# Batched matmul: x of two batches per transfer, the first x as one transfer, transposes of a pair in one block

## The chip, the cores and the metric

One Trainium2 chip, one core. The metric is the device time of one execution in microseconds (us). Most executions of a kernel agree within 0.3%. With one core there is no second die to compare, so slow runs would show only as runs over 1.5% above the fastest.

## The reference

```python
def setup_inputs():
    batch, m, k, n = 32, 512, 1024, 768
    return {"x": randn(batch, m, k).astype(float32), "weight": randn(batch, k, n).astype(float32)}

def reference(x, weight):
    return np.matmul(x, weight).astype(np.float32)
```

Per batch the kernel must read 2.10 MB of x and 3.15 MB of weights and write 1.57 MB of output: 218 MB in 32 batches.

## The kernel before

x and weights are loaded by transfers that cast float32 to bf16 on the way (issued by the GpSimd queue); the first x alone comes as float32, by the SyncE queue. A row group of x is 4 rows of one partition, 16 KB in memory; of the weights 8 rows, 24 KB. The TensorE transposes x in pairs of bf16 values taken as float32 words, the VectorE copies the result from PSUM to SBUF, and the matmuls follow. The parts that the change touches:

```python
x_pool  = ctx.enter_context(tc.tile_pool(name="x", bufs=5))
xT_pool = ctx.enter_context(tc.tile_pool(name="xT", bufs=8))
# ...
def load_x(b):
    xs[b] = x_pool.tile([P, MT, K], BF16, name="x_sb")
    nc.gpsimd.dma_start(out=xs[b], in_=x_view[b])

def transpose(b, mt):
    pt = tpsum.tile([P, JT, P], F32, name="pt")
    pairs = xs[b].bitcast(F32)
    for j in range(JT):
        nc.tensor.transpose(pt[:, j, :], pairs[:, mt, j::JT], ident)
    xT = xT_pool.tile([P, JT, P, 2], BF16, name="xT")
    nc.vector.tensor_copy(...)                     # contiguous
    return xT
# ...  the first x: three of four rows of each partition, then 18 small transfers
x_first = first_pool.tile([P, MT, K], F32)
nc.sync.dma_start(x_first[:, :MT - 1], x_view[0, :, :MT - 1])
at = 0
for few, times in ((4, 2), (5, 1), (6, 1)):
    for _ in range(times):
        for first in range(at, at + 4):
            rows = slice(first, at + 4 * few, 4)
            nc.sync.dma_start(x_first[rows, MT - 1], x_view[0, rows, MT - 1])
        at += 4 * few
for rows in (slice(at, 80), slice(80, P)):
    nc.sync.dma_start(x_first[rows, MT - 1], x_view[0, rows, MT - 1])
# ...  in the loop over batches: transposes stand between the matmul groups
xT = {mt: turn(b, mt) for mt in (0, 1)}
for pair in range(2):
    pm = banks()
    for half in range(2):
        if pair == 0:
            matmuls(pm, half, xT[half], b, range(KT), False)
            xT[2 + half] = turn(b, 2 + half)
        else:
            matmuls(pm, half, xT[2 + half], b, range(KT), False)
    evacuate(b, pair, pm)
```

The last outputs are held back and stored at the end, so that the DMA engines have work while the last batches are computed.

## Time and profile before

| | before |
|---|---|
| time, median (range) of the first 6 runs | 516.93 us (516.89 to 516.97) |
| profiled span | 515.2 us |
| TensorE busy | 81% |
| bytes moved at the memory | 218.1 MB, 423 GB/s over the span |
| first transpose | 33.6 us |
| last TensorE work ends | about 501.2 us |

Lines of the page of the kernel before. The three rows are the span in 40 slices, a digit being the busy share in tenths (PEclk: the granted TensorE clock); the last line sums the memory traffic.

```profile
PE   0039999999999988798978879977898978989980
PEclk9999999999999989799988997998997989999995
DMA  8999999999999999999999999999999999999996
HBM read 167.77 MB, written 50.33 MB: 423 GB/s over the span
```

The DMA row has no gap between the first and the last slice, while the TensorE, idle in the first two slices, is less than 90% busy in most slices from the fifteenth (180 us) on. The windows view of the kernel before says the same more finely. After the stretch and its length come the busy times of the engines, then the granted clock, the share of the DMA engines and GB/s.

```profile
100.00:200.00 100.00, 93.19 (x589) 61.67 (x588) 29.66 (x45) 16.98 (x29) 11.14 (x21) 0.98 1.02 270
200.00:300.00 100.00, 85.88 (x516) 55.69 (x515) 24.83 (x38) 15.22 (x26) 10.07 (x19) 0.93 1.02 263
300.00:400.00 100.00, 83.65 (x494) 53.73 (x493) 24.61 (x38) 14.05 (x24) 10.09 (x19) 0.91 1.02 263
505.00:514.00 9.00, 0.00 (x0) 0.00 (x0) 0.00 (x0) 0.00 (x0) 0.00 (x0) 0.50 0.64 267
```

The DMA share is 1.02: packets follow one another without a gap and overlap a little. Only the last stretch falls off, because the 16 engines do not end together.

What the TensorE waited for in the kernel before (us in total, times, longest us):

```profile
PE pm L101 <- DMA w_sb<-in_weight_dram: 44.0, 18, 4.0
PE pt L83 <- DMA x_first<-in_x_dram: 33.6, 1, 33.6
```

It starts late, at 33.6 us: the 18 small transfers of the first x are issued one after another until 25.0 us (the SyncE queue waited ten times, 12.5 us in all, for an earlier one to land), their packets of 172 ns come between weight packets of 926 ns, and the last one lands at 33.6 us. It then still waits 44 us for weights.

### The profile page before, as it was taken

Reading aid. Unit: us, or ns where it says so; the run is one execution under the profiler, and the core shown is the slowest. Engines: PE = TensorE matmul, PEld = TensorE weight load, DVE = VectorE, ACT = ScalarE, POOL = GpSimd, SP = SyncE. Lnnn points to the kernel's source line nnn. Section 1 sums busy time; section 2 is a strip of 40 time slices with the busy share of each in tenths; the row PEclk is TensorE's granted clock in tenths of the full one; section 3 lists DMA queues with packets and bytes.
Section 4 is the critical chain, followed back from the end, with each engine's and each line's share of the span. In section 5 each row is a group of like instructions: output and inputs, shape, how many; then the busy total and the mean of one; then the engine's idle time right before and its main releaser. Section 6 shows DMA issues by size and latency. Waiting matters only on the chain.

```text
span 515.2 us, 6001 instructions
## 1 busy us (share of the span) xinstructions
PE 419.6 (81%) x2576; PEld 275.7 (54%) x2576; DVE 129.8 (25%) x196; ACT 76.2 (15%) x129; POOL 51.7 (10%) x102
## 2 busy tenths in 40 slices
PE   0039999999999988798978879977898978989980
PEld 0026666666666655465645545654564645656650
DVE  0023333333333313133122231322331313332320
ACT  0001111111111101011111111110110111111110
POOL 3000111111000110100101001100111010111000
PEclk9999999999999989799988997998997989999995
DMA  8999999999999999999999999999999999999996
GB/s 233 223 225 220 209 278 277 260 238 276 274 276 267 237 269 276 275 272 245 254 276 275 276 254 243 273 278 275 266 239 265 276 276 274 240 253 213 291 430 272
DMA packets 15081, 135.64 MB, mean 263 GB/s; under 512 B 1744, under 2 KB 1744, under 8 KB 3536
## 3 DMA queue, kind: packets, MB, share of 16 engines
q0 software_dynamic: 13824, 126.88, 96.7%
q1 hardware_dynamic: 1232, 8.39, 4.1%
q8 instruction: 20, 0.33, 0.2%
q14 instruction: 5, 0.04, 0.0%
HBM read 167.77 MB, written 50.33 MB: 423 GB/s over the span
## 4 chain that ended last, share of the span: by engine, by line
DMA 69%; PE 25%; DVE 2%; issue 1%; ACT 0%; POOLq 0%
DMA w_sb<-in_weight_dram 31%; PE pm L101 22%; DMA out_dram<-out_sb 16%; DMA x_sb<-in_x_dram 15%; DMA x_first<-in_x_dram 6%; PE pt L70 2%; PE pt L83 1%; DVE out_sb L113 1%; DVE xT L72 1%; ACT out_sb L112 0%; ACT out_sb L114 0%; POOLq L62 0%; POOLq L148 0%; POOLq L56 0%
## 5 line engine op out<-in xcount | busy, mean ns | idle before, releaser
L101 PE MATMUL pm<-w_sb,xT 128*128 128x256 bf16 (+1 forms) x2048 | 364.7, 336 | 47.9 <-DMA w_sb<-in_weight_dram 44.0
L101 PEld LDWEIGHTS <-xT 128*128 128x128 bf16 x2048 | 203.3, 100 | 184.6 <-issue 50.5
L72 DVE COPY xT<-pt 128x1024 bf16<-128x1024 bf16 x124 | 82.8, 689 | 203.0 <-PE pt L70 203.0
L112 ACT COPY out_sb<-pm 128x512 f32<-128x512 f32 x64 | 37.5, 585 | 286.7 <-PE pm L101 286.7
L70 PEld LDWEIGHTS pt<-ident,x_sb 128*128 128x128 f32 x496 | 72.9, 206 | 6.3 <-issue 1.3
L113 DVE COPY out_sb<-pm 128x512 f32<-128x512 f32 x64 | 44.0, 687 | 128.1 <-PE pm L101 128.1
L70 PE MATMUL pt<-ident,x_sb 128*128 128x128 f32 x496 | 75.4, 286 | 0.0
L114 ACT COPY out_sb<-pm 128x512 f32<-128x512 f32 x64 | 37.5, 586 | 138.2 <-PE pm L101 138.0
L62 POOL DMA_DIRECT2D w_sb<-in_weight_dram x37 | 19.8, 534 | 154.9 <-PE pm L101 74.6
L56 POOL DMA_DIRECT2D x_sb<-in_x_dram x31 | 16.5, 532 | 173.4 <-DMA w_sb<-in_weight_dram 129.4
L83 PE MATMUL pt<-ident,x_first 128*128 128x128 f32 x32 | 6.0, 350 | 33.6 <-DMA x_first<-in_x_dram 33.6
L148 POOL DMA_DIRECT2D out_dram<-out_sb x28 | 15.0, 536 | 93.2 <-DMA x_sb<-in_x_dram 55.9
L83 PEld LDWEIGHTS pt<-ident,x_first 128*128 128x128 f32 x32 | 5.0, 204 | 34.3 <-issue 33.6
L84 DVE CAST xT<-pt 128x512 bf16<-128x512 f32 x8 | 5.6, 726 | 40.7 <-PE pt L83 40.5
L112 ACT ACT_TABLE_LOAD x1 | 1.3, 1283 | 0.7 <-PEq L199 0.7
masks.py:199 POOL TENSOR_SCALAR_AFFINE_SELECT ident<-ident 128x128 f32<-128x128 f32 x1 | 0.3, 287 | 0.1
masks.py:197 POOL MEMSET ident<- 128x128 f32 x1 | 0.2, 223 | 0.0
L199 POOL MEMSET const-float32-0.0<- 128x1 f32 x1 | 0.1, 98 | 0.2 <-issue 0.2
L199 POOL MEMSET const-bfloat16-1.0<- 128x1 bf16 x1 | 0.1, 101 | 0.0
L199 POOL MEMSET const-uint8-127<- 128x1 uint8 x1 | 0.1, 101 | 0.0
L199 POOL MEMSET const-float32-1.0<- 128x1 f32 x1 | 0.1, 98 | 0.0
## 6 DMA issues: line engine op xcount, KB each, us to landing
w_sb<-in_weight_dram POOLq DMA_DIRECT2D x28, 1536.0 KB, 43.2
out_dram<-out_sb POOLq DMA_DIRECT2D x28, 1536.0 KB, 42.0
x_sb<-in_x_dram POOLq DMA_DIRECT2D x31, 1024.0 KB, 39.6
w_sb<-in_weight_dram POOLq DMA_DIRECT2D x7, 768.0 KB, 31.9
out_dram<-out_sb SPq DMA_DIRECT2D x4, 768.0 KB
out_dram<-out_sb SPq DMA_DIRECT2D x2, 1536.0 KB
x_first<-in_x_dram SPq DMA_DIRECT2D x1, 1536.0 KB
w_sb<-in_weight_dram POOLq DMA_DIRECT2D x2, 384.0 KB, 28.6
```

The source lines that it names most:

```text
L56: nc.gpsimd.dma_start(out=xs[b], in_=x_view[b])
L62: nc.gpsimd.dma_start(out=ws[b][:, at:at + n, :], in_=w_view[b, :, at:at + n, :])
L70: nc.tensor.transpose(pt[:, j, :], pairs[:, mt, j::JT], ident)
L72: nc.vector.tensor_copy(xT.rearrange("p j m r -> p (j m r)"), pt.bitcast(BF16).rearrange("p j m -> p (j m)"))
L83: nc.tensor.transpose(pt[:, i, :], x_first[:, mt, JT * h + i::KT], ident)
L84: nc.vector.tensor_copy(xT[:, 2 * h:2 * h + 2].rearrange("p j m r -> p j r m"), pt.rearrange("p (j r) m -> p j r m", r=2),)
L101: nc.tensor.matmul(pm[bank][:, at:at + size], xT[:, ko // 2, :, ko % 2], ws[b][:, ko, off:off + size], start=(ko == 0 and not (together an ...
L112: nc.scalar.copy(o[:, 0:512], pm[0])
L113: nc.vector.tensor_copy(o[:, 512:1024], pm[1])
L114: nc.scalar.copy(o[:, 1024:N2], pm[2])
L148: nc.gpsimd.dma_start(out=out_view[at], in_=outs[at])
L199: nc = _bacc.Bacc("TRN2", target_bir_lowering=False, num_devices=1)
```

## The change

The intent: fewer and longer transfers. One transfer loads x of two batches, 8 rows (32 KB) per partition, so that a partition holds rows of only one of the two batches; a transposed tile then has columns of both. The first x comes in one transfer and lies in one of the three pair buffers; the last batch keeps a transfer and transposes of its own (cut below, as is the order of the first loads). All transposes of a pair now come in one block before the odd batch's matmuls, and the copies write 4-byte words 8 bytes apart.

```diff
-    x_pool = ctx.enter_context(tc.tile_pool(name="x", bufs=5))
-    xT_pool = ctx.enter_context(tc.tile_pool(name="xT", bufs=8))
+    x_pool = ctx.enter_context(tc.tile_pool(name="x", bufs=3))
+    xT_pool = ctx.enter_context(tc.tile_pool(name="xT", bufs=6))
+    pair_view = x[1:B - 1].rearrange("(p r) (mi mo) k -> p (r mi) mo k", r=2, mo=2 * MT)
-    def load_x(b):
-        xs[b] = x_pool.tile([P, MT, K], BF16, name="x_sb")
-        nc.gpsimd.dma_start(out=xs[b], in_=x_view[b])
+    def load_pair(b):
+        xs[b] = x_pool.tile([P, 2 * MT, K], BF16, name="x_sb")
+        nc.gpsimd.dma_start(out=xs[b], in_=pair_view[b // 2])
+    def transpose_pair(b, mt):
+        both = xT_pool.tile([P, 2, JT, P // 2, 2, 2], BF16, name="xT")
+        for half in range(2):
+            nc.vector.tensor_copy(
+                both[:, :, :, :, half, :].rearrange("p b j i r -> p j b i r"),
+                words(b, mt + MT * half).rearrange("p j (b i r) -> p j b i r", b=2, r=2),
+            )
+        return [both[:, r].rearrange("p j i h r -> p j (i h) r") for r in range(2)]
     # ...
-        nc.sync.dma_start(x_first[:, :MT - 1], x_view[0, :, :MT - 1])
-        # ... 18 small transfers
+        x_first = x_pool.tile([P, MT, K], F32, name="x_sb")
+        nc.sync.dma_start(x_first, x_view[0])
     # ... in the loop
+                if b % 2:
+                    for mt in range(MT):
+                        ready[b, mt], ready[b + 1, mt] = transpose_pair(b, mt)
+                xT = {mt: ready.pop((b, mt)) for mt in range(MT)}
             # ... then the matmuls, with no transposes between them
```

More of the change, by code (lines that the diff above doesn't have):

```diff
@@ L34 @@
     const = ctx.enter_context(tc.tile_pool(name="const", bufs=1))
-    first_pool = ctx.enter_context(tc.tile_pool(name="first", bufs=1))
     w_pool = ctx.enter_context(tc.tile_pool(name="w", bufs=4))
-    x_pool = ctx.enter_context(tc.tile_pool(name="x", bufs=5))
-    xT_pool = ctx.enter_context(tc.tile_pool(name="xT", bufs=8))
+    x_pool = ctx.enter_context(tc.tile_pool(name="x", bufs=3))
+    xT_pool = ctx.enter_context(tc.tile_pool(name="xT", bufs=6))
     out_pool = ctx.enter_context(tc.tile_pool(name="out", bufs=7))
@@ L52, in banks, with load_last @@
         return [mpsum.tile([P, 512], F32, name=f"pm{i}") for i in range(3)]
-    def load_x(b):
-        xs[b] = x_pool.tile([P, MT, K], BF16, name="x_sb")
-        nc.gpsimd.dma_start(out=xs[b], in_=x_view[b])
+    def load_pair(b):
+        xs[b] = x_pool.tile([P, 2 * MT, K], BF16, name="x_sb")
+        nc.gpsimd.dma_start(out=xs[b], in_=pair_view[b // 2])
+    def load_last():
+        xs[B - 1] = x_pool.tile([P, MT, K], BF16, name="x_sb")
+        nc.gpsimd.dma_start(out=xs[B - 1], in_=x_view[B - 1])
     def load_w(b):
@@ L63, in load_w, with words @@
             at += n
-    def transpose(b, mt):
+    def words(b, mo):
         pt = tpsum.tile([P, JT, P], F32, name="pt")
@@ L69, in transpose, with transpose_last @@
         for j in range(JT):
-            nc.tensor.transpose(pt[:, j, :], pairs[:, mt, j::JT], ident)
+            nc.tensor.transpose(pt[:, j, :], pairs[:, mo, j::JT], ident)
+        return pt.bitcast(BF16)
+    def transpose_pair(b, mt):
[6 more added lines that the diff above has]
+        return [both[:, r].rearrange("p j i h r -> p j (i h) r") for r in range(2)]
+    def transpose_last(mt):
         xT = xT_pool.tile([P, JT, P, 2], BF16, name="xT")
         nc.vector.tensor_copy(
-            xT.rearrange("p j m r -> p (j m r)"), pt.bitcast(BF16).rearrange("p j m -> p (j m)")
+            xT.rearrange("p j m r -> p (j m r)"), words(B - 1, mt).rearrange("p j m -> p (j m)")
         )
@@ L116 @@
     with tc.manual_schedule():
-        x_first = first_pool.tile([P, MT, K], F32)
-        nc.sync.dma_start(x_first[:, :MT - 1], x_view[0, :, :MT - 1])
-        at = 0
-        for few, times in ((4, 2), (5, 1), (6, 1)):
-            for _ in range(times):
-                for first in range(at, at + 4):
-                    rows = slice(first, at + 4 * few, 4)
-                    nc.sync.dma_start(x_first[rows, MT - 1], x_view[0, rows, MT - 1])
-                at += 4 * few
-        for rows in (slice(at, 80), slice(80, P)):
-            nc.sync.dma_start(x_first[rows, MT - 1], x_view[0, rows, MT - 1])
+        x_first = x_pool.tile([P, MT, K], F32, name="x_sb")
+        nc.sync.dma_start(x_first, x_view[0])
         load_w(0)
@@ L131 @@
         make_identity(nc, ident)
-        for b in range(1, AHEAD):
-            load_x(b)
-            load_w(b)
-        load_x(AHEAD)
+        load_pair(1)
+        load_w(1)
+        load_w(2)
+        load_pair(3)
+        ready = {}
         pending = []
         for b in range(B):
-            if b + AHEAD + 1 < B:
-                load_x(b + AHEAD + 1)
+            if b % 2 and b + AHEAD + 1 < B:
+                if b + AHEAD + 1 == B - 1:
+                    load_last()
+                else:
+                    load_pair(b + AHEAD + 1)
             if b + AHEAD < B:
@@ L156 @@
             outs[b] = out_pool.tile([P, MT * N], F32, name="out_sb")
+            if b == 0:
+                xT = {mt: transpose_first(mt) for mt in range(MT)}
+            elif b == B - 1:
+                xT = {mt: transpose_last(mt) for mt in range(MT)}
+            else:
+                if b % 2:
+                    for mt in range(MT):
+                        ready[b, mt], ready[b + 1, mt] = transpose_pair(b, mt)
+                xT = {mt: ready.pop((b, mt)) for mt in range(MT)}
             if b not in CHUNKED:
-                turn = transpose if b else lambda _, mt: transpose_first(mt)
-                xT = {mt: turn(b, mt) for mt in (0, 1)}
                 for pair in range(2):
@@ L162 @@
                     for half in range(2):
-                        if pair == 0:
-                            matmuls(pm, half, xT[half], b, range(KT), False)
-                            xT[2 + half] = turn(b, 2 + half)
-                        else:
-                            matmuls(pm, half, xT[2 + half], b, range(KT), False)
+                        matmuls(pm, half, xT[2 * pair + half], b, range(KT), False)
                     evacuate(b, pair, pm)
                 continue
-            xT = {0: transpose(b, 0)}
             pms = [banks() for _ in range(2)]
@@ L175 @@
                 for mt in range(MT):
-                    if mt + 1 not in xT and mt + 1 < MT:
-                        xT[mt + 1] = transpose(b, mt + 1)
                     matmuls(pms[mt // 2], mt % 2, xT[mt], b, range(at, at + n), True)
```

## The prediction

> **What bounds the kernel now.** Data transfer. In the page's 40 slices the DMA row reads 9 from the second slice to the second last; 10 us windows show the 16 DMA engines booked 1.02 of the time from 10 us to 490 us and 1.01 to 500 us. The TensorE is busy 81%. HBM traffic is 167.8 MB read and 50.3 MB written, 423 GB/s over 515.2 us. The trace's casting packets cost their bytes: 6 KB read takes 248 ns, 12 KB 474, 16 KB (an x row group) 625, 24 KB (a weight row group) 926. That is 37.7 ns per KB plus about 22 ns, most of which overlaps the next packet (the booking of 1.02). So the bytes, which the change leaves alone, are nearly the whole time. The TensorE starts at 33.6 us, when the last small piece of the first x lands (chain of waits), runs 12.8 us per batch, catches up near 130 us and then waits for weights.
>
> **What the change removes, adds and moves.**
> - 15 pairs of x transfers become 15 single ones. Per pair and engine 8 packets of 32 KB replace 16 of 16 KB: at most 8 x 22 ns, 2.7 us over 15 pairs; with the overlap I estimate 0.7 to 1 us. Fifteen completions less: some 0.3 us.
> - The first x comes as one 2 MB transfer. I expect it at 8 to 15 us, so the TensorE starts about 20 us earlier. That buys slack, not time: the DMA engines were busy there anyway.
> - [...]At the end the engines run dry between 508 and 513 us[...].
> - All eight transpose groups of a pair now stand before the odd batch's matmuls. The VectorE sets the pace there: 8 copies of about 0.69 us (the present copy), some 6 us in which the TensorE does only 4 us of transposes. Per pair I estimate 20.8 us of matmuls at full clock (8 groups of 2.6 us), about 22 at the granted 0.95, plus 6.5: 28 to 29 us. The DMA needs 32.2 us per pair (2 x 16.1). Still DMA-bound.
> - The copies now write 4-byte words 8 bytes apart. The Trainium skill (SBUF — State Buffer, Specifications) gives 16-byte lines that need two hits for full bandwidth; this pattern has exactly two, so I expect 0.69 to 0.75 us. No copy of this trace has the pattern. At 1.05 us a pair would come to some 32 us and touch the DMA bound; at 1.4 us it would pass it.
>
> **On the critical path:** only the DMA bookkeeping, 1 us saved, and the tail, plus or minus 1 us. The last batches have no interleaved transposes, so the TensorE ends some 2 us later than 501.2 us, still hidden behind held stores that drain until about 509 us.
>
> **Predicted:** 516.0 us, 8 times in 10 between 512.5 and 519.5. Faster by over 2%: 0.02; within 2%: 0.93; slower by over 2%: 0.05.
>
> **What would show each step right:** DMA row still 9 throughout; x packets of about 1.23 us; first transpose at 8 to 15 us; pair copies near 0.7 us in runs of eight; TensorE waiting for weights about once per pair; last matmul between 501 and 506 us; last store packets ending near 512 us.
>
> **What would make it wrong:** slow strided copies (over 1.1 us), making TensorE and VectorE the bound; long x transfers that leave weights late because transfers are issued only after the eighth before them has landed (the queue's waits show it); or 32 KB packets costing more per byte than 16 KB ones.

## The result, and the profile after

516.35 us median of six runs (516.08 to 517.87), against 516.93 us (516.89 to 516.97). The ratio is 0.9997 (95% interval 0.9982 to 1.0012): the same. The changed kernel's six runs spread over 1.8 us, those of before over 0.1 us. A ratio here is the mean time of one kernel's fast runs over that of the other's of the same rounds, so not quite the ratio of the medians. The changed kernel ran unaltered in ten further runs (below); over all sixteen the median is 516.37 us and the mean 516.65 us.

The profile after is of a run of 517.87 us, one of the two long ones. Its lines that answer to those of before:

```profile
PE   0999979879799798988969979898897979999991
PEclk9999999979899798998979979999898997999997
DMA  8999999999999999999999999999999999999996
HBM read 167.77 MB, written 50.33 MB: 423 GB/s over the span
```

The DMA row is digit for digit that of before, and so is the traffic. The PE row has moved: work begins in the second slice. The windows view after:

```profile
100.00:200.00 100.00, 85.39 (x489) 53.14 (x487) 24.00 (x37) 14.10 (x25) 7.99 (x15) 0.91 1.01 262
200.00:300.00 100.00, 83.40 (x481) 52.40 (x482) 24.22 (x37) 14.63 (x25) 8.53 (x16) 0.93 1.02 268
300.00:400.00 100.00, 89.18 (x504) 55.24 (x503) 23.75 (x36) 14.66 (x25) 9.07 (x17) 0.92 1.02 264
505.00:514.00 9.00, 0.60 (x4) 0.10 (x1) 0.69 (x1) 1.05 (x2) 0.00 (x0) 0.81 0.73 303
```

The TensorE's waits after:

```profile
PE pm L120 <- DMA w_sb<-in_weight_dram: 42.3, 12, 5.5
PE pt L102 <- DMA x_sb<-in_x_dram: 12.2, 1, 12.2
PE pt L76 <- DVE xT L83: 10.1, 45, 0.3
```

The first x lands at 12.2 us instead of 33.6, and the TensorE waits about as long for weights as before, in fewer and longer stops (12 in place of 18). The third line is the pace of the VectorE in the block of transposes: 10.1 us in all. One pair of batches on the TensorE after, from the timeline (start, length, engine, line, what, idle time before it):

```profile
74.85 10.57 PE L120 MATMUL pm<-w_sb,xT 128*128 128x512 bf16 x64 [2.90 <-DMA w_sb<-in_weight_dram]
85.27 1.12 PE L76 MATMUL pt<-ident,x_sb 128*128 128x128 f32 x8
86.68 1.35 PE L76 MATMUL pt<-ident,x_sb 128*128 128x128 f32 x8 [0.30 <-DVE xT L83]
88.21 1.35 PE L76 MATMUL pt<-ident,x_sb 128*128 128x128 f32 x8 [0.18 <-DVE xT L83]
89.74 1.35 PE L76 MATMUL pt<-ident,x_sb 128*128 128x128 f32 x8 [0.18 <-DVE xT L83]
90.93 10.56 PE L120 MATMUL pm<-w_sb,xT 128*128 128x512 bf16 x64
106.96 3.38 PE L120 MATMUL pm<-w_sb,xT 128*128 128x512 bf16 x10 [5.47 <-DMA w_sb<-in_weight_dram]
```

From 74.85 to 106.96 us is one pair: 32.1 us, of which 5.5 us are waiting for the next even batch's weights. That wait is the longest of the twelve; eleven pairs later (same view, window 390:516) the last of them ends:

```profile
426.31 13.36 PE L120 MATMUL pm<-w_sb,xT 128*128 128x512 bf16 x64 [3.39 <-DMA w_sb<-in_weight_dram]
```

So these eleven pairs take 31.95 us each on average, of which 3.6 us are waiting ((42.3 - 2.9) / 11) and 28.4 us work. The transposes of the pair shown take 5.7 us in their block (85.27 to 90.93). On the VectorE the same block looks like this:

```profile
85.94 1.29 DVE L83 COPY xT<-pt 128x1024 bf16<-128x1024 bf16 x2
87.46 1.29 DVE L83 COPY xT<-pt 128x1024 bf16<-128x1024 bf16 x2 [0.24 <-PE pt L76]
88.99 1.30 DVE L83 COPY xT<-pt 128x1024 bf16<-128x1024 bf16 x2 [0.24 <-PE pt L76]
90.53 1.30 DVE L83 COPY xT<-pt 128x1024 bf16<-128x1024 bf16 x2 [0.24 <-PE pt L76]
```

The groups view gives the copies' mean before and after, 689 and 687 ns: writing words 8 bytes apart costs nothing visible.

```profile
L72 DVE COPY xT<-pt 128x1024 bf16<-128x1024 bf16 x124 | 82.8, 689 | 203.0 <-PE pt L70 203.0
```

```profile
L83 DVE COPY xT<-pt 128x1024 bf16<-128x1024 bf16 x120 | 77.4, 687 | 10.9 <-PE pt L76 10.9
```

The trace also lists each packet of the DMA engines with its duration. Median ns of the main kinds and the sum of all packets over 32 bytes, divided by 16 engines:

```text
                                before    after    changed kernel again (r_after)
x packet, 16 KB read               625      625      625   (after: the last batch only)
x packet, 32 KB read                 -     1227     1227
weight packet, 24 KB read          926      926      926
store packet, 12 KB                460      460      460
sum per engine, us               518.6    517.6    516.6
packets longer than their kind      23      151       81
the profiled run took, us       517.03   517.87   516.17
engines end between, us   508.0, 513.1  509.6, 514.8  508.4, 513.2
```

(Longer than their kind: of the GpSimd queue's packets from 25 us on, weight packets over 960 ns, store packets over 500, x packets over 660 or 1260 ns. The engines' ends are read by stringing each packet to the one it follows; a string may change engines on the way, its end does not depend on that.)

### The profile page after: what moved, and what is told of

It reads as the page before. It is cut to its first block, busy times and chain, and to the rows that moved or that the text cites. A ratio compares the mean times of both kernels' runs of the same rounds, so it can differ in the third digit from the quotient of the medians.

```text
span 516.1 us, 5820 instructions
## 1 busy us (share of the span) xinstructions
PE 440.4 (85%) x2576; PEld 279.7 (54%) x2576; DVE 129.8 (25%) x196; ACT 76.3 (15%) x129; POOL 44.0 (9%) x87
## 4 chain that ended last, share of the span: by engine, by line
PE 64%; DMA 21%; DVE 7%; another core or an unknown queue 6%; issue 1%; ACT 0%
PE pm L120 56%; DMA w_sb<-in_weight_dram 18%; PE pt L76 6%; DVE xT L83 4%; DMA x_sb<-in_x_dram 2%; DVE out_sb L132 2%; PE pt L102 1%; DVE xT L103 0%; DVE xT L91 0%; ACT out_sb L133 0%
## 5 line engine op out<-in xcount | busy, mean ns | idle before, releaser
L120 PE MATMUL pm<-w_sb,xT 128*128 128x256 bf16 (+1 forms) x2048 | 359.5, 339 | 42.3 <-DMA w_sb<-in_weight_dram 42.3
L120 PEld LDWEIGHTS <-xT 128*128 128x128 bf16 x2048 | 206.8, 101 | 190.3 <-DMA w_sb<-in_weight_dram 46.9
L76 PE MATMUL pt<-ident,x_sb 128*128 128x128 f32 x496 | 79.8, 303 | 10.4 <-DVE xT L83 10.1
L76 PEld LDWEIGHTS pt<-ident,x_sb 128*128 128x128 f32 x496 | 69.3, 209 | 21.4 <-DVE xT L83 18.6
L83 DVE COPY xT<-pt 128x1024 bf16<-128x1024 bf16 x120 | 77.4, 687 | 10.9 <-PE pt L76 10.9
L102 PE MATMUL pt<-ident,x_sb 128*128 128x128 f32 x32 | 6.5, 355 | 12.6 <-DMA x_sb<-in_x_dram 12.2
L102 PEld LDWEIGHTS pt<-ident,x_sb 128*128 128x128 f32 x32 | 5.1, 205 | 13.7 <-issue 12.2
L58 POOL DMA_DIRECT2D x_sb<-in_x_dram x15 | 8.0, 535 | 45.1 <-DMA out_dram<-out_sb 31.0
L91 DVE COPY xT<-pt 128x1024 bf16<-128x1024 bf16 x4 | 2.6, 686 | 0.2 <-PE pt L76 0.2
L62 POOL DMA_DIRECT2D x_sb<-in_x_dram x1 | 0.5, 530 | 6.9 <-DMA w_sb<-in_weight_dram 6.9
```

The source lines that it names most:

```text
L58: nc.gpsimd.dma_start(out=xs[b], in_=pair_view[b // 2])
L76: nc.tensor.transpose(pt[:, j, :], pairs[:, mo, j::JT], ident)
L83: nc.vector.tensor_copy(both[:, :, :, :, half, :].rearrange("p b j i r -> p j b i r"), words(b, mt + MT * half).rearrange("p j (b i r) -> ...
L91: nc.vector.tensor_copy(xT.rearrange("p j m r -> p (j m r)"), words(B - 1, mt).rearrange("p j m -> p (j m)"))
L102: nc.tensor.transpose(pt[:, i, :], x_first[:, mt, JT * h + i::KT], ident)
L120: nc.tensor.matmul(pm[bank][:, at:at + size], xT[:, ko // 2, :, ko % 2], ws[b][:, ko, off:off + size], start=(ko == 0 and not (together an ...
```

## The experiments

Eleven runs were made (two of the unaltered changed kernel), in three groups; those of a group shared one chip and the runs of before (median 516.91 us in each group, 516.87 to 517.17).

### r_after and r_after2: the changed kernel again, unaltered

> The changed kernel once more, unaltered, for its spread. Of its first six runs four took 516.1 to 516.4 us and two 517.87; before took 516.89 to 516.97 in all six. If the two levels are a property of the kernel (DMA engines that end unevenly), both come back: most near 516.2, some near 517.9, and before stays within 0.1 us. If the two long runs were chance of the machine, all should be near 516.2. A profile at the lower level should show the last packets ending about 1.7 us earlier than the 514.8 us of the profile at hand.

Measured: 516.24 us median (516.12 to 516.93), ratio 0.9989 (0.9977 to 1.0002). The profile is of a 516.17 us run; the engines end 1.7 us earlier than in the 517.87 us run.

> The changed kernel unaltered, beside the one with moved transposes on the same chip, and for its spread: medians near 516.3 us, single runs between 516.1 and 517.9 us. Before: 516.9 within 0.2 us.

Measured: 516.89 us (516.20 to 517.35), ratio 0.9996 (0.9984 to 1.0009). What follows: there are not two levels but a spread from 516.1 to 517.9 us, which the kernel before does not have. The times of the profiled runs of this kernel go with the number of long packets: 81 at 516.17 us, 108 at 517.35, 151 at 517.87. Most of them are weight packets. That is a correlation over three profiles; what makes them long was not found.

### e_one_first: only the first x as one transfer, in the kernel before

```diff
-        nc.sync.dma_start(x_first[:, :MT - 1], x_view[0, :, :MT - 1])
-        # ... 18 small transfers
+        nc.sync.dma_start(x_first, x_view[0])
```

> The kernel before with only one part of the change: the first x as one 2 MB transfer in place of one large and 18 small ones. My theory (the DMA engines' bytes set the time): the first transpose moves from 33.6 us to about 12 us, and the time stays at 516 to 518 us, perhaps now with two levels as the changed kernel has. Rival (the TensorE's late start lies on the path): 495 to 505 us. Second question: if the small transfers evened out the engines' ends, this kernel shows a spread of over 0.5 us between its runs, and its time rises by 0 to 1 us.

Measured: 517.14 us (516.87 to 517.88), ratio 1.0005 (0.9993 to 1.0018). The TensorE's waits in this kernel:

```profile
PE pm L101 <- DMA w_sb<-in_weight_dram: 61.1, 25, 4.0
PE pt L83 <- DMA x_first<-in_x_dram: 12.2, 1, 12.2
```

The TensorE starts 21.4 us earlier and waits 17.1 us longer for weights (61.1 against 44.0). The head start is handed back in waiting. The rival, that the late start lay on the path, is refuted. The second question was answered with yes: this kernel's five runs spread over 1.0 us, so the spread appears without the pairs, with the single first transfer alone. That this transfer causes it is not shown: e_small_back below has the spread without it.

### e_half_mm and e_half_mm_less_out: take matmuls away, then bytes

```diff
-        for ko in kos:
+        for ko in [ko for ko in kos if ko % 2 == 0 or ko == KT - 1]:
```

> The changed kernel with three of every eight matmul steps left out (5/8 of the matmuls, the result is wrong on purpose); all transfers, transposes and copies stay. Theory (the bytes on the DMA engines set the time): 515 to 517 us, though the TensorE's work falls by some 120 us. Rival (the TensorE chain sets it, as 64% of the chain of waits being TensorE may suggest): under 480 us.

Measured: 515.56 us (514.80 to 516.15), ratio 0.9972 (0.9957 to 0.9987); the result is wrong, as intended. TensorE busy time fell from 440 to 323 us, and the time by 0.8 us (medians; 1.1 us by the means, against all sixteen runs of the changed kernel). The first lines of the two pages, after and here:

```profile
PE 440.4 (85%) x2576; PEld 279.7 (54%) x2576; DVE 129.8 (25%) x196; ACT 76.3 (15%) x129; POOL 44.0 (9%) x87
```

```profile
PE 323.3 (63%) x1776; PEld 207.8 (41%) x1808; DVE 130.3 (25%) x196; ACT 76.2 (15%) x129; POOL 43.8 (9%) x87
```

So the TensorE is not what sets the time, although 64% of the chain of waits after is put down to it:

```profile
PE 64%; DMA 21%; DVE 7%; another core or an unknown queue 6%; issue 1%; ACT 0%
```

The second kernel leaves out the stores of eight batches as well:

```diff
-                        nc.gpsimd.dma_start(out=out_view[at], in_=outs[at])
+                        if not 4 <= at < 12:
+                            nc.gpsimd.dma_start(out=out_view[at], in_=outs[at])
```

> As the kernel with 5/8 of the matmuls, and the stores of batches 4 to 11 left out (8 of 32 outputs stay unwritten, wrong on purpose): 12.6 MB less. Theory: each store is 8 packets per engine of about 455 ns, so 29 us less: 486 to 489 us. A rival that puts the time on anything other than bytes moved expects less than 5 us of change.

Measured: 486.19 us (485.61 to 486.73), 29.4 us less than with the stores, where 29 us were expected from the packets alone. With the TensorE relieved, bytes move the time one for one; matmuls hardly move it. What the full kernel would gain from fewer bytes was not run: its TensorE has only 42.3 us of waiting to give up.

### e_split_pair: each pair as two transfers

```diff
-        nc.gpsimd.dma_start(out=xs[b], in_=pair_view[b // 2])
+        for rows in (slice(0, MT), slice(MT, 2 * MT)):
+            nc.gpsimd.dma_start(out=xs[b][:, rows], in_=pair_view[b // 2, :, rows])
```

> The changed kernel with each pair's x loaded as two transfers of four rows per partition: the packets are 16 KB read again (625 ns) and there are 15 more transfers, all else as changed. Theory: 0.7 to 1.3 us more than the changed kernel, since per pair and engine 16 packets replace 8. Rival (a packet's 22 ns is all hidden): within 0.2 us of it. If the 22 ns were paid in full: 2.7 to 3.3 us more.

Measured: 516.66 us (516.39 to 517.93) against 516.24 us for r_after on the same chip; the means are 516.98 and 516.40. So about 0.4 to 0.6 us, below the 0.7 to 1.3 us that I expected, and not clear of the spread. The sum of packets per engine went from 516.6 to 518.8 us, yet the time moved by about a quarter of these 2.2 us or less; that the rest is overlap is likely, but not shown. The full price of 22 ns a packet is refuted; that the price is zero is not.

### e_small_back: the small first transfers put back

The first x loaded as in the kernel before, all else as changed (the diff above, reversed).

> The changed kernel with the first x loaded as before did (one large and 18 small transfers). Theory: first transpose at about 33 us again, time 515.5 to 516.5 us, and the level near 517.9 us does not occur if the small transfers even out the engines. Rival (the early start of the TensorE was needed to carry the transposes that are no longer interleaved): 520 us or more.

Measured: 517.20 us (517.00 to 519.16), ratio 1.0006 (0.9992 to 1.0020). The first transpose came at 40.5 us in the profiled run, later than the 33 us that I expected; the time is above the expected 515.5 to 516.5 us, and the spread stayed (that profile is of the slowest run, 519.16 us). So the small transfers do not narrow the spread here, and they cost about 1 us against r_after on the same chip (no run of the one reaches into the range of the other). The rival (520 us or more) is refuted for all but its mildest form: even a start at 40 us is carried.

### e_double_copy: the copies done twice

```diff
+            turned = words(b, mt + MT * half)
-            nc.vector.tensor_copy(...)
+            for _ in range(2):
+                nc.vector.tensor_copy(...)     # the same copy, the same place
```

> The changed kernel with every copy of a transposed pair tile done twice (same source, same place, correct result), as if the strided copies were twice as slow: 8 more copies of 0.645 us per pair, 5.2 us. In the changed kernel's trace a pair takes the TensorE 26.5 us at full clock, some 27.6 at the granted clock, and the DMA engines 32.2. So theory: the slack is 4.5 to 5.7 us per pair and this kernel sits right at it or over it: 517 to 536 us. If the slack was much larger than I think: 516 us. If there was none: 590 us.

Measured: 527.86 us (527.47 to 527.92), ratio 1.0209 (1.0194 to 1.0225). The DMA row of its page, and the first lines of the TensorE's waits:

```profile
DMA  8999999999999999999999999999999999999756
```

```profile
PE pt L76 <- DVE xT L85: 45.1, 90, 1.1
PE pt L104 <- DMA x_sb<-in_x_dram: 12.2, 1, 12.2
```

The wait for weights has gone; it was all the slack there was. The changed kernel has 42.3 us of it, that is 2.8 us per pair over all 15 pairs and 3.6 us on average in the eleven pairs measured above, and not the 4.5 to 5.7 us that I wrote for this run. Doubling the copies lengthens the block of one pair from 5.7 to 9.8 us (125.26 to 135.07 us in its timeline), 4.1 us more, an estimated 62 us over 15 pairs, of which the waits could take up 42; the TensorE then ends about 15 us later, at about 520.8 us, and the DMA engines wait for it at the end.

### e_pitch: what a word's distance costs

```diff
+            if mt < 2 and b > 1:     # scratch copies of 128 words, 4, 8 and 16 bytes apart
+                nc.vector.tensor_copy(spread(1), turned[:, 0].rearrange("p (i r) -> p i r", r=2))
+                nc.vector.tensor_copy(spread(2), turned[:, 0].rearrange("p (i r) -> p i r", r=2))
+                nc.vector.tensor_copy(spread(4), turned[:, 0].rearrange("p (i r) -> p i r", r=2))
```

> The changed kernel with three more copies by the VectorE out of half of the transposed tiles of each pair from the second on, each 256 bf16 values per partition, written into a scratch tile as 4-byte words side by side, 8 bytes apart and 16 bytes apart. If 16-byte lines with at least two hits run at full rate (the Trainium skill, SBUF - State Buffer, Specifications): the first two take the same time, about 0.29 us (512 words take 0.69, so an estimate of 0.16 fixed plus 128 words), and the third 0.08 to 0.2 us more. If single words 8 bytes apart already cost: the second is 0.08 us or more above the first. The whole is expected 1 to 12 us slower, as the copies lengthen the pair's transpose block by some 3.5 us.

Measured: 519.07 us (one run). The groups view of the three copies, L92 with words side by side, L93 8 bytes apart, L94 16 bytes apart:

```profile
L94 DVE COPY scratch<-pt 128x256 bf16<-128x256 bf16 x56 | 21.4, 382 | 1.9
L93 DVE COPY scratch<-pt 128x256 bf16<-128x256 bf16 x56 | 16.4, 292 | 1.9
L92 DVE COPY scratch<-pt 128x256 bf16<-128x256 bf16 x56 | 15.4, 275 | 0.0
```

8 bytes apart costs 17 ns (6%) for 128 words, 16 bytes apart 107 ns. But for these 17 ns, this agrees with what the Trainium skill says (SBUF — State Buffer, Specifications): lines of 16 bytes, two hits each for full bandwidth. The layout of the change stands just on the right side of that step. From the slope between the last two, (382 - 292) / 128 = 0.7 ns a word, a full copy of 512 words at 16 bytes would take an estimated 0.36 us longer, 2.9 us per pair: as much as the pair waits on average (2.8 us over 15 pairs).

### e_hoist: half of the transposes moved into the wait

```diff
+                elif b >= 4 and b + 1 < B - 1:
+                    for mt in range(2):
+                        ready[b + 1, mt], ready[b + 2, mt] = transpose_pair(b + 1, mt)
```

> The changed kernel with half of the next pair's transposes (two of four tiles, as many as the six xT buffers allow) moved ahead of the even batch's matmuls, where the TensorE waits 2.5 to 5.4 us for weights. Theory: the time does not move beyond 0.7 us (515.5 to 516.4), since the DMA engines' bytes set it; the TensorE's waits for weights fall below 25 us in total (42.3 in the changed kernel) and its last matmul ends 1 to 4 us before 505.6 us. If the late TensorE still held the last stores back, as the 0.7 us gained with 5/8 of the matmuls may suggest, up to 0.7 us faster than the changed kernel of the same rounds. Rival (the transposes standing in one block cost time): 3 us or more faster.

Measured: 516.26 us (516.13 to 517.67), ratio 0.9991 (0.9977 to 1.0004); the changed kernel in the same rounds 516.89 us. The two spreads cover each other. The last matmul ended at about 502.1 us against 505.0 in r_after2, so 2.9 us earlier, as expected, and the time did not follow. The wait for weights did not fall below 25 us; it stayed at 41.9:

```profile
PE pm L120 <- DMA w_sb<-in_weight_dram: 41.9, 11, 4.9
```

That expectation was badly reasoned: while the DMA engines set the pace, work moved into a wait only makes the TensorE wait at the next weights.

### e_even_0to7: the first x in five transfers, to even out the engines' ends

```diff
-        nc.sync.dma_start(x_first, x_view[0])
+        for rows in (slice(0, 96), slice(96, 104), slice(104, 112), slice(112, 120), slice(120, P)):
+            nc.sync.dma_start(x_first[rows], x_view[0, rows])
```

> The changed kernel with the first x in five transfers: 96 rows, then four times 8 rows. If a transfer of 8 rows goes to 8 of the 16 engines (the Trainium skill, DMA: Bandwidth and Descriptors, says the lowest-numbered), those eight get 10 packets and the others 6[...]. At the lower level of the changed kernel eight engines end at 508.4 to 509.6 us and eight at 511.3 to 513.2. If the eight that get more are the early ones: 0.8 to 1.5 us faster than the changed kernel, about 515 us, all engines ending within 2.5 us. If they are the late ones: about 1.2 us slower. If unevenness of ends isn't what ends the program: within 0.3 us.

Measured: 523.31 us (522.59 to 524.08), ratio 1.0123 (1.0108 to 1.0138), outside all three expectations. The first transpose came at 26.4 us, and the 128 packets of the first x took 1143 ns on average against 731 in r_after. Summed over all packets, each engine was booked 6 us longer than in r_after (522.5 against 516.6), most of it in packets that started in the first 30 us. So this split slows the transfers themselves, and it does so for all five: the first 96 of the 128 packets, in order of start, took 1048 ns on average (767 in r_after), the last 32, those of the four transfers of 8 rows, 1428 ns (624), and the 32 KB packets of x that started before 30 us 1441 ns (1227). The large transfer still landed 11.2 us after its issue (the whole 2 MB in r_after: 11.4):

```profile
x_sb<-in_x_dram SPq DMA_DIRECT2D x1, 1536.0 KB, 11.2
x_sb<-in_x_dram SPq DMA_DIRECT2D x4, 128.0 KB
```

The four small ones, issued by 2.6 us, were complete only at 26.4 us. Why is not shown. The late start is not what costs the time: e_small_back starts at 40.5 us and takes 517.20 us. The bytes are the same and the time is 7 us longer: it is the time that packets take, and not their bytes as such, that sets it. The question that the run was to answer, which engines end late, stays open: the ends still spread over 4.2 us (515.4 to 519.6), and the profile's packets carry no engine number, so the numbering that the expectation takes from the Trainium skill was not seen either.

## Why the prediction was right

- **DMA-bound, bytes unchanged: right.** The DMA share is 1.01 to 1.02 in the 100 us windows after, as before. Taking matmuls away moved the time by about 1 us, taking 12.6 MB away by 29.4 us. What sets a packet's time, the engine or the memory, no run here tells.
- **The first x earlier, no time gained: right.** 12.2 us (8 to 15 predicted). e_one_first shows the head start turning into 17.1 us more waiting for weights.
- **Merged x packets, about 1 us saved: shown in the packets, not in the time.** 32 KB packets took 1227 ns (1.23 us predicted). Leave out what long packets took beyond their kind's median (0.3, 2.2 and 1.0 us per engine in the table's columns), and the sums are 518.3, 515.4 and 515.6 us: some 2.8 us less booked, near the 2.7 us that 120 packets of 22 ns come to. Little of this reached the time. Over all sixteen runs the mean is 0.3 us below that of before (516.65 against 516.92 to 516.96), at the lower end of the spread it is 0.8 us; e_split_pair puts the merge at 0.4 to 0.6 us; none of it is clear of the spread. Part of the saving is eaten by packets that took longer than their kind, 81 to 151 against 23; their cause is open.
- **The block of transposes fits: right.** 5.7 us per block (6 told). From 74.85 to 426.31 us a pair took 31.95 us (32.2 told), with 28.4 us of work (28 to 29 estimated) and 3.6 us of waiting.
- **Copies at full rate: right.** 687 ns, and e_pitch shows where the step lies. The warning that slow copies would turn the bound was also right: e_double_copy took 527.9 us.
- **The tail: nearly right.** The last matmul ended at about 505.6 us (501 to 506 predicted). The last packets ended at 513.2 to 514.8 us and not near 512; e_half_mm, with a TensorE that is done some 13 us earlier, gains about 1 us, so the later TensorE is not wholly hidden, or the spread favours it; e_hoist, at 2.9 us earlier, shows nothing clear of the spread.
- **The number: partly luck.** 516.35 us is 0.35 us from the 516.0 told, but the runs spread over 1.8 us, which was not foreseen and is more than the whole saving forecast. What the prediction earned is the bound and the "same", not the tenths.

No version with a correct result is clearly faster than either kernel. e_hoist (516.26 us) has a median as low as the changed kernel's, inside the spread.

## What to carry to other kernels

Here the DMA engines were booked without a gap, and an earlier start (21 us) and moved work (2.9 us) turned into waiting elsewhere. What counted was the time of the packets: nearly their bytes, but not in e_even_0to7, where the same bytes took 7 us longer. A test that removes compute and one that removes bytes show such a bound in two runs. Before you rely on slack, read it from the waits for the bounding resource (42.3 us here, 3.6 us in a pair that waits), not from a difference of two estimates. The chain of waits may name the engine that ended last for 64% of the time and still not name the bound.

## What the Trainium skill lacked or had wrong

- DMA: Bandwidth & Descriptors gives a fixed cost of about 2 us for each transfer (section on the anatomy of one DMA) and advises to merge. It lacks what a merge is worth when the queue never runs empty: 15 transfers and 8 packets per pair and engine fewer were worth about 0.4 to 0.6 us in all, not clear of the spread, though each packet carries about 22 ns beyond its bytes.
- SBUF — State Buffer, Specifications, was neither lacking nor wrong, but for 17 ns: 275, 292 and 382 ns for 128 words 4, 8 and 16 bytes apart.
- Vector Engine (DVE) Microarchitecture Reference, section on measured stream behaviour, asks for runs of two adjacent words for full rate. For the bf16 copy from PSUM here, single words 8 bytes apart cost only 17 ns on 275. The page's table has 32-bit streams and larger hops; for this copy its rule does not hold as worded.
- Left open by the runs, and not tested against any page: why packets of one kind sometimes take longer (23 in one kernel's profile, 81 to 151 in the other's), which engines end late (a spread of some 5 us), and why the five transfers of e_even_0to7 made packets of 16 KB take 1143 ns on average instead of 731.
